# Neighbourhood attention on Trainium2: queries stored rotated by 64 tokens, one unit of work for a whole head

## The chip, the cores and the metric

The kernel is written for one Trainium2 chip and runs on one of its cores. A core has five engines that run at once and meet only through semaphores: TensorE (PE, matrix products and transposes into PSUM; its weight loads are shown as PEld), VectorE (DVE), ScalarE (ACT), GpSimd (POOL) and SyncE (SP, which here issues nearly all transfers). PSUM has eight banks of 2 KB for each of 128 partitions. The metric is the device time of one execution in microseconds, the median of several runs.

## The reference

The model is an encoder of two layers with 512 tokens of width 1024. In each layer three mixers work on the same normalised input: differential attention, a convolution and a two-dimensional neighbourhood attention. Their outputs are gated and merged, and a feed-forward block and a gated embedding follow. The change lies in the neighbourhood attention alone. It sees the 512 tokens as 8 rows of 64 columns; a query at column w attends to all 8 rows, but only to 16 columns around it:

```python
cs = jnp.clip(cols - NA_KC // 2, 0, GRID_W - NA_KC)      # NA_KC = 16, GRID_W = 64
...
s = jnp.einsum('bhwd,bhrwcd->bhwrc', q_r, kn).astype(jnp.float32) * scale
s = s + bias.transpose(0, 2, 1, 3)[None].astype(jnp.float32)
a = jax.nn.softmax(s.reshape(B, HC, GRID_W, KR * NA_KC), axis=-1)
return jnp.einsum('bhwrc,bhrwcd->bhwd', a, vn)
```

There are 8 heads of width 64, and the bias depends on head, row distance and column distance. All is float32.

## The kernel before, in words

Tokens are kept in the order column by column (token = column x 8 + row), so that the 16 columns that a query may see are 128 neighbouring tokens in that order, and a tile of 128 queries (16 columns) sees at most 256 keys. Products that must keep float32 accuracy are made of two or three faster ones: a value is split into a rounded part (by ACT) and the remainder (by DVE), `split` at L162.

PE's instruction order is the order of the program, written by hand. The other engines' orders are laid out by a scheduler that takes what is ready by priority; each queue is then fixed. The dense projections are the bulk of PE's work: `gemm` (L181) multiplies a weight block of 128 x 1024, 8 chunks of three matmuls of 512 columns (L177 to L179), and calls `chunk` after each; every fourth chunk is a tick (L94). The attention's work is cut into generators, called units, that wait in a queue: at a tick, units whose time has come do their next step, and a new unit starts when the one before it has left the gap that `later` gives it (L107). So the short work of a unit stands between ticks' worth of projections.

For each pair of heads `natten_in` (L634) projects queries and keys, makes rounded part and remainder, and has `stack` (L656) copy them by SP's transfers into `st4` and `k2`, where the two parts lie above each other in the partitions, so that two matmuls (`scores`, L809) give a full product. `natten_v` (L665) makes the values of all heads, and at its end copies two 64-token edges of the values into tiles `vd` of their own (L688 to L695).

`natten_unit` (L697) takes two query tiles of one head, so that a head has two units (`half` 0 and 1). The first step makes for each of the two tiles a score tile of 128 x 256 in a PSUM tile `sc` of its own (of two buffers), then DVE adds the bias and takes the maximum (L712, into the bias tile `b`), ACT takes the exponential into `e` with its sum, and after a reciprocal ACT scales `e`. Two of the four query tiles begin their 256 keys at a multiple of 128 tokens (0 and 256), the two in the middle do not (`KEY0` = 0, 64, 192, 256), and those have a 64-column margin of zeros in `e`, written by POOL (L720). Two ticks later the second step transposes the probabilities: five transposes of 128 x 128, the fifth for the edge, into two PSUM tiles that are split into `pp` and `p2`. Two ticks later the third step multiplies by the values: four products of 256 columns with two aligned value tiles and one of 128 columns with the edge tile `vd` (L756), and the output goes into `y`.

Of the kernel before, what the change touches and what calls it, by code (L numbers as in the profile page):

```python
# [11 lines left out]
F32 = mybir.dt.float32  # L12
F32R = mybir.dt.float32r
# [22 lines left out]
KEY0 = (0, 64, 192, 256)  # L36
# [25 lines left out]
class Net:  # L62
# [571 lines left out]
    def natten_in(self, pr, st, ys):  # L634
# [4 lines left out]
        for s, off in enumerate((OFF_QC, OFF_KC)):  # L639
# [16 lines left out]
    def stack(self, nat, low, one, two):  # L656

        for n, part in enumerate((nat, low)):
            for st, r in ((one, 64 * n), (two, 64 - 64 * n)):
                for u in range(2):  # L660
                    if st is not None:
                        self.nc.sync.dma_start(st[r:r + 64, u].bitcast(F32),
                                               part[64 * u:64 * u + 64].bitcast(F32))

    def natten_v(self, st):  # L665
# [31 lines left out]
    def natten_unit(self, pr, half, u, st4, k2, st, y):  # L697

        nc, i = self.nc, self.i
        mm = nc.tensor.matmul  # L700
        head = 2 * pr + u
        b = self.sb("b", [P, 2, NW])
# [3 lines left out]
        m = self.sb("s", [P, 6])  # L706
        for t in range(2):
            qt = 2 * half + t
            sc = self.ps("sc", (P, NW))
            self.scores(sc, st4, k2, u, slice(qt * P, (qt + 1) * P),  # L710
                        slice(KEY0[qt], KEY0[qt] + NW))
            nc.vector.tensor_tensor_reduce(  # L712
                out=b[:, t], in0=sc, in1=b[:, t], scale=-1.0, scalar=3.0e38,
                op0=ALU.add, op1=ALU.min, accum_out=m[:, t:t + 1])
            wide = half != t
            e = self.sb("e", [P, NW + 64 * wide])
            own = slice(64 * (qt == 1), 64 * (qt == 1) + NW)
            if wide:
                pad = slice(0, 64) if qt == 1 else slice(NW, NW + 64)
                nc.gpsimd.memset(e[:, pad], 0.0)  # L720
            self.act(e[:, own], b[:, t], AF.Exp, table="exp", scale=-1.0, bias=m[:, t:t + 1],
                     accum_out=m[:, 2 + t:3 + t])
            es.append((e, e[:, own]))
        nc.vector.reciprocal(m[:, 4:6], m[:, 2:4])
        for t, (_, own) in enumerate(es):
            self.act(own, own, AF.Copy, scale=m[:, 4 + t:5 + t])
        yield 2
        pt = self.ps("tr", (P, 2, 256))
        pt2 = self.ps("tr", (P, P))
        p2 = self.sb("a", [P, P], F32R)  # L730
        for t, (e, _) in enumerate(es):
            qt = 2 * half + t
            c0 = 64 * (qt == 2)
            ts = slice(t * P, (t + 1) * P)
            if qt == 2:
                nc.tensor.transpose(pt2, e[:, 0:P], self.ident)
            for c in range(2):
                nc.tensor.transpose(pt[:, c, ts], e[:, c0 + c * P:c0 + (c + 1) * P], self.ident)
            if qt == 1:
                nc.tensor.transpose(pt2, e[:, NW - 64:NW + 64], self.ident)  # L740
            if half != t:
                ws = ts
        pp = self.sb("pt", [P, 2, 2, 256], F32R)
        self.split(pp[:, 0], pp[:, 1], pt)

        er, eo = (slice(0, 64), slice(64, P))[::1 if half else -1]
        self.split(p2[er], p2[eo], pt2[er])
        yield 2
        vs, vd = st["v", pr // 2]
        av = self.ps(("av", "mm")[u], (P, 256))  # L750
        hc = (pr % 2) * 256 + u * P
        cols = slice(hc, hc + P)
        for n in range(2):
            for k in range(2):
                mm(av, vs[half][:, n, cols], pp[:, k, n], start=n == k == 0, stop=False)
        mm(av[:, ws], vd[:, half, cols], p2, start=False, stop=True)  # L756


        qs = slice(half * 256, half * 256 + 256)
        rs, ro = (slice(0, 64), slice(64, P))[::-1 if u else 1]  # L760
        self.split(y[rs, 0, qs], y[rs, 1, qs], av[rs])
        self.tt(y[rs, 1, qs], y[rs, 1, qs].bitcast(F32), av[ro], ALU.add)
# [46 lines left out]
    def scores(self, out, st4, k2, u, qs, ks):  # L809


        for n, st in enumerate((st4[:, 2 + u], k2[:, u])):
            self.nc.tensor.matmul(out, st4[:, u, qs], st[:, ks], start=n == 0, stop=n == 1)  # L813
# [678 lines left out]
```

## Time and profile before

| | |
|---|---|
| median of 3 runs | 1781.01 us (1780.66 to 1782.22) |
| span of the profiled execution, first to last instruction | 1778.5 us (the page gives no other time of this execution; the median is 2.5 us more) |
| instructions | 27425, of them 10210 matmuls |
| PE / DVE / ACT busy | 1768.7 / 1376.2 / 915.0 us |
| DMA | 256.04 MB, 144 GB/s on average |
| mean granted TensorE clock | 0.999 |

Busy time is the time in which an engine has at least one instruction in hand. Matmuls overlap in the pipeline of PE, so that the distance between two starts, not the printed duration, is what one costs. In timelines the columns are start (us), duration (us), engine, line, operation, written tile <- read tiles, shape, count, and in brackets the idle time before it with what ended it; in the view of windows, the busy time of each engine (with its instructions), granted clock, share of the DMA engines and GB/s. "natten", "diff", "glu" and so on in tile names are the phases of the program.

### The profile page before, as it was taken

To read this page: it belongs to the slowest core of one execution; us is meant where nothing else is said; L and a number is where in the kernel's file an instruction comes from. 1 tells how busy PE (TensorE), PEld (TensorE's weight loads), DVE (VectorE), ACT (ScalarE), POOL (GpSimd) and SP (SyncE) were. 2 spreads that over 40 slices of the span, in tenths; PEclk is the share of its full clock that TensorE was granted. 3 is DMA by queue.
4 is the path that set the end of the run, shared out by engine and by line. 5 is a ranking of instruction groups with operands and counts; after the bars stand their busy time and mean duration, and the time that the engine had idled before them with its cause. 6 is when DMAs were issued, how large, how long until landed. Compare 5 with 4: busy or idle time off the path is not lost.

```text
span 1778.5 us, 27425 instructions
## 1 busy us (share of the span) xinstructions
PE 1768.7 (99%) x10210; PEld 1559.0 (88%) x10210; DVE 1376.2 (77%) x2284; ACT 915.0 (51%) x1607; POOL 108.8 (6%) x146
## 2 busy tenths in 40 slices
PE   9999999999999999999999999999999999999998
PEld 7888888888899899998888888888888998989987
DVE  7878887998787576777776788889887875766676
ACT  5577545325576254454545765452356652634544
POOL 0000000000121010100000000000001210101000
PEclk9999999999999999999999999999999999999999
DMA  5666541334767365543447655423256663655332
GB/s 210 188 183 171 161 125 44 111 98 146 224 160 182 116 168 152 141 121 126 141 127 197 177 166 149 113 71 95 94 177 197 173 178 112 176 140 154 99 104 95
DMA packets 113507, 256.04 MB, mean 144 GB/s; under 512 B 14560, under 2 KB 19424, under 8 KB 113376
## 3 DMA queue, kind: packets, MB, share of 16 engines
q1 hardware_dynamic: 99984, 229.93, 42.2%
q0 software_dynamic: 12672, 23.07, 7.8%
q8 instruction: 80, 1.31, 0.3%
q10 hardware_dynamic: 720, 1.31, 0.2%
q14 instruction: 51, 0.42, 0.1%
HBM read 215.46 MB, written 7.34 MB: 125 GB/s over the span
## 4 chain that ended last, share of the span: by engine, by line
PE 95%; DVE 2%; ACT 1%; issue 1%; DMA 0%; POOL 0%; ACTq 0%; POOLq 0%; DVEq 0%
PE ffn_mm L177 4%; PE ffn_mm L178 4%; PE ffn_mm L179 4%; PE ffn_mm L1022 3%; PE ffn_mm L1020 3%; PE ffn_mm L1021 3%; PE ffn_sc L1020 3%; PE ffn_sc L1022 3%; PE ffn_sc L1021 3%; PE mergea_mm L179 2%; PE mergea_mm L177 2%; PE mergea_mm L178 2%; PE diff_sc L813 2%; PE gatec_mm L177 2%; PE gatec_mm L178 2%; PE gatec_mm L179 2%
## 5 line engine op out<-in xcount | busy, mean ns | idle before, releaser
L160 DVE SCALAR_TENSOR_TENSOR conv_z<-glu_z,pre_par,conv_z 128x512 f32<-128x512 f32 x240 | 179.6, 748 | 3.3
L143 ACT ACTIVATE ffn_wh<-ffn_wr 128x1024 fp32r<-128x1024 f32 (+1 forms) x92 | 93.4, 1021 | 140.2 <-PE ffn_mm L178 75.3
L157 DVE TENSOR_TENSOR ffn_wl<-ffn_wr,ffn_wh 128x1024 fp32r<-128x1024 f32 (+1 forms) x92 | 107.6, 1175 | 40.7 <-ACT ffn_wh L143 40.3
L990 POOL DMA_DIRECT2D ffn_qk<-w_fu x88 | 78.0, 961 | 601.7 <-DMA ffn_qk<-w_fu 336.4
L157 DVE TENSOR_TENSOR ffn_t<-ffn_mm,wo_rb 128x512 f32<-128x512 f32 (+1 forms) x86 | 47.8, 556 | 71.0 <-PE ffn_mm L179 60.7
L143 ACT ACTIVATE mergea_wh<-mergea_wr 128x1024 fp32r<-128x1024 f32 (+1 forms) x32 | 27.1, 846 | 96.8 <-PE mergea_mm L178 79.5
L157 DVE TENSOR_TENSOR ffn_wl<-ffn_qk,ffn_wh 128x1024 fp32r<-128x1024 f32 x44 | 53.9, 1224 | 15.5 <-ACT ffn_wh L143 15.5
L143 ACT ACTIVATE ffn_wh<-ffn_qk 128x1024 fp32r<-128x1024 f32 x44 | 46.6, 1060 | 33.3 <-PE ffn_mm L178 16.1
L143 ACT ACTIVATE diff_a<-diff_sc,diff_s 128x512 f32<-128x512 f32 x32 | 22.0, 687 | 61.0 <-DVE diff_s L905 61.0
L177 PE MATMUL ffn_mm<-ffn_v,ffn_wh 128*128 128x512 f32 x132 | 51.4, 389 | 0.0
L178 PE MATMUL ffn_mm<-ffn_v,ffn_wh 128*128 128x512 f32 x132 | 51.4, 389 | 0.0
L179 PE MATMUL ffn_mm<-ffn_v,ffn_wl 128*128 128x512 f32 x132 | 51.3, 389 | 0.0
L177 PE MATMUL ffn_mm<-ffn_y,ffn_wh 128*128 128x512 f32 x132 | 51.3, 389 | 0.0
L178 PE MATMUL ffn_mm<-ffn_y,ffn_wh 128*128 128x512 f32 x132 | 51.3, 389 | 0.0
L179 PE MATMUL ffn_mm<-ffn_y,ffn_wl 128*128 128x512 f32 x132 | 51.3, 389 | 0.0
L1020 PE MATMUL ffn_mm<-wo_h,ffn_wh 128*128 128x256 f32 x176 | 49.9, 284 | 0.0
L1021 PE MATMUL ffn_sc<-wo_h,ffn_wh 128*128 128x256 f32 x176 | 49.8, 283 | 0.0
L1022 PE MATMUL ffn_mm<-wo_h,ffn_wl 128*128 128x256 f32 x176 | 49.8, 283 | 0.0
L1022 PE MATMUL ffn_sc<-wo_h,ffn_wl 128*128 128x256 f32 x176 | 49.8, 283 | 0.0
L1020 PE MATMUL ffn_sc<-wo_h,ffn_wh 128*128 128x256 f32 x176 | 49.8, 283 | 0.0
L1021 PE MATMUL ffn_mm<-wo_h,ffn_wh 128*128 128x256 f32 x176 | 49.8, 283 | 0.0
L143 ACT ACTIVATE natten_wh<-natten_wr 128x1024 fp32r<-128x1024 f32 x24 | 25.4, 1058 | 41.4 <-issue 15.2
(868 smaller groups left out, 6548.5 us busy)
## 6 DMA issues: line engine op xcount, KB each, us to landing
ffn_qk<-w_fu POOLq DMA_DIRECT2D x88, 256.0 KB, 6.5
ffn_wr<-w_fg SPq DMA_DIRECT2D x44, 512.0 KB, 4.2
ffn_wr<-w_fd SPq DMA_DIRECT2D x32, 448.0 KB, 3.9
ffn_r<-w_fu SPq DMA_DIRECT2D x44, 256.0 KB, 3.2
ffn_qk<-w_fg SPq DMA_DIRECT2D x44, 256.0 KB, 2.9
ffn_qk<-w_fu SPq DMA_DIRECT2D x44, 256.0 KB, 3.2
natten_wr<-w_in SPq DMA_DIRECT2D x16, 512.0 KB, 4.4
natten_b<-bias SPq DMA_DIRECT2D x32, 256.0 KB, 4.0
```

What stands on the lines that cost most here:

```text
L143: i = self.nc.scalar.activation(out, in_, func, **kw)
L157: return self.nc.vector.tensor_tensor(out, a, b, op)
L160: return self.nc.vector.scalar_tensor_tensor(out, a, s, b, op0, op1)
L177: mm(out, wh, ah, start=first, stop=False, **kw)
L178: mm(out, wh, al, start=False, stop=False, **kw)
L179: mm(out, wl, ah, start=False, stop=last, **kw)
L813: self.nc.tensor.matmul(out, st4[:, u, qs], st[:, ks], start=n == 0, stop=n == 1)
L990: nc.gpsimd.dma_start(q, wu[:, lo], accum_op=ALU.add)
L1020: mm(out, wh[:, c], bh, start=first and k == 0, stop=False, skip_group_check=True)
L1021: mm(out, wh[:, c], bl, start=False, stop=False, skip_group_check=True)
L1022: mm(out, wl[:, c], bh, start=False, stop=k == 3, skip_group_check=True)
```

## The change

Queries are stored rotated by 64 tokens (`MOVE`): tile q of the rotated order holds tokens 128 q - 64 to 128 q + 63, taken round the end. A tile then needs two key tiles of 128 that begin at multiples of 128: tiles q - 1 and q for q = 1, 2, 3, and tiles 0 and 3 for q = 0, which holds the first and the last 64 tokens. The bias table is laid out to match, on the host. There are no edge tiles any more, neither of values (`vd`) nor of probabilities (`p2`), and no margins.

- `stack` writes the queries in two pieces each (448 and 64 columns), the keys as before.
- A unit takes a whole head; a pair of heads has two units with a gap of two ticks instead of four with a gap of one. Its second step comes three ticks after the first, instead of two, and the third two ticks after that.
- The first step makes four score tiles, two in each PSUM tile `sc` of 2 x 256, that is one 2 KB bank; only the first product into a bank starts an accumulation. DVE's work on tile t = 0 stands in the program ahead of the scores of t = 1. The exponential is written over the biased scores, in the bias tile. The second bias tile of a unit has the tag `e`, of which there are four buffers; the first has `b`, with two.
- The second step makes eight transposes into two PSUM tiles of four. The third makes eight value products, two for each key tile, of 192, 256, 256 and 192 columns, into one PSUM tile of 512 columns in the order of the tokens (so the rotation ends here), and one split of 64 x 512.
- `scores` takes a function that picks the keys; for tile 0 it is the first and the last 128 of 512.

```diff
-KEY0 = (0, 64, 192, 256)
+MOVE = 64
...
-            self.stack(nat, low, st4[:, 2 * s:2 * s + 2], k2 if s else None)
+            self.stack(nat, low, st4[:, 2 * s:2 * s + 2], k2 if s else None, 0 if s else MOVE)
         ys.append(self.sb("y", [P, 2, 512], F32R))
-        for n in range(4):
-            self.later(self.natten_unit(pr, n // 2, n % 2, st4, k2, st, ys[pr]), 6 if pr == 3 else 5 if pr else 10, 1)
+        for u in range(2):
+            self.later(self.natten_unit(pr, u, st4, k2, st, ys[pr]), 6 if pr == 3 else 5 if pr else 10, 2)
...
+        cols = (slice(0, 512 - move), slice(move, 512)), (slice(512 - move, 512), slice(0, move))
...
+                    for src, dst in cols[:1 + (move > 0)]:
+                        if st is not None:
+                            self.nc.sync.dma_start(st[r:r + 64, u, dst].bitcast(F32),
+                                                   part[64 * u:64 * u + 64, src].bitcast(F32))
...
-        for g in range(2):
-            vd = self.sb("x", [P, 2, 512], F32R)
-            for n, edge in enumerate((vs[g][1][0:64, 0], vs[g][0][64:P, 1])):
-                for o in range(0, P, 64):
-                    self.nc.sync.dma_start(vd[o:o + 64, n].bitcast(F32), edge.bitcast(F32))
-            st["v", g] = vs[g], vd
+        st.update(enumerate(vs))
...
+        bs = [self.sb(t, [P, 2, NW]) for t in ("b", "e")]
         with self.tc.high_priority(offset=100):
-            nc.sync.dma_start(b, self.a["bias"][i, head, half])
+            for half, b in enumerate(bs):
+                nc.sync.dma_start(b, self.a["bias"][i, head, half])
...
+        for half, b in enumerate(bs):
+            sc = self.ps("sc", (P, 2, NW))
+            for t in range(2):
+                qt = 2 * half + t
+                keys = (lambda a, qt=qt: a[:, qt * P - P:qt * P + P]) if qt else \
+                    (lambda a: a.rearrange("p (a b) -> p a b", b=P)[:, 0::3])
+                self.scores(sc[:, t] if qt else sc[:, t].rearrange("p (a b) -> p a b", b=P),
+                            st4, k2, u, slice(qt * P, (qt + 1) * P), keys, t == 0,
+                            skip_group_check=True)
+                es.append(b[:, t])
+                nc.vector.tensor_tensor_reduce(
+                    out=b[:, t], in0=sc[:, t], in1=b[:, t], scale=-1.0, scalar=3.0e38,
+                    op0=ALU.add, op1=ALU.min, accum_out=m[:, qt:qt + 1])
+                self.act(b[:, t], b[:, t], AF.Exp, table="exp", scale=-1.0, bias=m[:, qt:qt + 1],
+                         accum_out=m[:, 4 + qt:5 + qt])
+            c = slice(4 + 2 * half, 6 + 2 * half)
+            nc.vector.reciprocal(m[:, c], m[:, c])
+            for t in range(2):
+                self.act(b[:, t], b[:, t], AF.Copy, scale=m[:, c][:, t:t + 1])
+        yield 3
+        ps = []
+        for half in range(2):
+            pt = self.ps("tr", (P, 4, P))
+            for n in range(4):
+                kc, q = 2 * half + n // 2, (2 * half + (n + 1) // 2) % 4
+                c = (kc != q - 1 if q else kc == 3) * P
+                nc.tensor.transpose(pt[:, n], es[q][:, c:c + P], self.ident)
+            pp = self.sb("pt", [P, 2, 512], F32R)
+            self.split(pp[:, 0], pp[:, 1], pt.rearrange("p a b -> p (a b)"))
+            ps.append(pp)
         yield 2
...
+        for kc, (o, n, c) in enumerate(((0, 192, MOVE), (MOVE, 256, 256), (192, 256, 0), (320, 192, 256))):
             for k in range(2):
-                mm(av, vs[half][:, n, cols], pp[:, k, n], start=n == k == 0, stop=False)
-        mm(av[:, ws], vd[:, half, cols], p2, start=False, stop=True)
+                mm(av[:, o:o + n], vs[kc // 2][:, kc % 2, hc:hc + P], ps[kc // 2][:, k, c:c + n],
+                   start=kc == k == 0, stop=kc == 3 and k == 1, skip_group_check=True)
...
-    def scores(self, out, st4, k2, u, qs, ks):
+    def scores(self, out, st4, k2, u, qs, keys, first=True, **kw):
         for n, st in enumerate((st4[:, 2 + u], k2[:, u])):
-            self.nc.tensor.matmul(out, st4[:, u, qs], st[:, ks], start=n == 0, stop=n == 1)
+            self.nc.tensor.matmul(out, st4[:, u, qs], keys(st), start=first and n == 0, stop=n == 1, **kw)
```

More of the change, by code (lines that the diff above doesn't have):

```diff
@@ L701, in natten_unit @@
         head = 2 * pr + u
-        b = self.sb("b", [P, 2, NW])
+        bs = [self.sb(t, [P, 2, NW]) for t in ("b", "e")]
         with self.tc.high_priority(offset=100):
-            nc.sync.dma_start(b, self.a["bias"][i, head, half])
+            for half, b in enumerate(bs):
+                nc.sync.dma_start(b, self.a["bias"][i, head, half])
+        m = self.sb("s", [P, 8])
         es = []
[L706 to L723, printed above, removed]
@@ L724, in natten_unit @@
-        nc.vector.reciprocal(m[:, 4:6], m[:, 2:4])
-        for t, (_, own) in enumerate(es):
-            self.act(own, own, AF.Copy, scale=m[:, 4 + t:5 + t])
-        yield 2
[L728 to L750, printed above, removed]
+        for half, b in enumerate(bs):
[17 more added lines that the diff above has]
+                self.act(b[:, t], b[:, t], AF.Copy, scale=m[:, c][:, t:t + 1])
@@ L751, in natten_unit @@
+        yield 2
+        av = self.ps(("av", "mm")[u])
         hc = (pr % 2) * 256 + u * P
-        cols = slice(hc, hc + P)
-        for n in range(2):
+        vs = st[pr // 2]
+        for kc, (o, n, c) in enumerate(((0, 192, MOVE), (MOVE, 256, 256), (192, 256, 0), (320, 192, 256))):
             for k in range(2):
-                mm(av, vs[half][:, n, cols], pp[:, k, n], start=n == k == 0, stop=False)
-        mm(av[:, ws], vd[:, half, cols], p2, start=False, stop=True)
-        qs = slice(half * 256, half * 256 + 256)
+                mm(av[:, o:o + n], vs[kc // 2][:, kc % 2, hc:hc + P], ps[kc // 2][:, k, c:c + n],
+                   start=kc == k == 0, stop=kc == 3 and k == 1, skip_group_check=True)
@@ L760, in natten_unit @@
         rs, ro = (slice(0, 64), slice(64, P))[::-1 if u else 1]
-        self.split(y[rs, 0, qs], y[rs, 1, qs], av[rs])
-        self.tt(y[rs, 1, qs], y[rs, 1, qs].bitcast(F32), av[ro], ALU.add)
+        self.split(y[rs, 0], y[rs, 1], av[rs])
+        self.tt(y[rs, 1], y[rs, 1].bitcast(F32), av[ro], ALU.add)
     def gate_c(self, acc, m):
@@ L903, in probs @@
             sc = self.ps("sc")
-            self.scores(sc, st4, k2, u, qs, slice(0, 512))
+            self.scores(sc, st4, k2, u, qs, lambda a: a)
             nc.vector.tensor_reduce(out=m[:, u:u + 1], in_=sc, op=ALU.max, axis=AX.X, negate=True)
```

12 lines of the change are left out of this document (5 added, 7 removed).

## The prediction

> **What bounds the kernel now.** I read the profile's page first.
>
> ```profile
> span 1778.5 us, 27425 instructions
> ...
> PE 1768.7 (99%) x10210; PEld 1559.0 (88%) x10210; DVE 1376.2 (77%) x2284; ACT 915.0 (51%) x1607; POOL 108.8 (6%) x146
> ...
> PE 95%; DVE 2%; ACT 1%; issue 1%; DMA 0%; POOL 0%; ACTq 0%; POOLq 0%; DVEq 0%
> ```
>
> TensorE (PE) is busy 99% of the span and is 95% of the chain that ended last. A busy PE need not be a fast one, so I looked next for time in which it waits. In the list of PE's waits these are the two largest that concern other engines in mid-kernel (total us, times, longest):
>
> ```profile
> PE ffn_mm L1022 <- DVE ffn_pt L157: 2.0, 2, 1.0
> ...
> PE natten_tr L738 <- ACT natten_e L143: 0.3, 2, 0.2
> ```
>
> So next to nothing is lost to waiting, least of all in the neighbourhood attention (natten), and what decides is how long PE's own instruction stream is, plus any wait that the change puts into it. VectorE (DVE), ScalarE (ACT) and the queues matter only where PE waits for them. For PE I use the distance from one start to the next, since the printed durations overlap. The timeline of PE around the first natten units (start us, us):
>
> ```profile
> 83.35 0.60 PE L738 MATMUL natten_tr<-pre_ident,natten_e 128*128 128x128 f32 x4
> 83.78 0.27 PE L740 MATMUL natten_tr<-pre_ident,natten_e 128*128 128x128 f32 x1
> 83.81 0.36 PE L813 MATMUL natten_sc<-natten_qk 128*128 128x256 f32 x1
> 84.01 0.28 PE L813 MATMUL natten_sc<-natten_x,natten_qk 128*128 128x256 f32 x1
> ...
> 84.25 0.28 PE L813 MATMUL natten_sc<-natten_x,natten_qk 128*128 128x256 f32 x1
> 84.37 0.39 PE L177 MATMUL glu_mm<-glu_h,glu_wh 128*128 128x512 f32 x1
> 84.60 0.39 PE L178 MATMUL glu_mm<-glu_h,glu_wh 128*128 128x512 f32 x1
> ...
> 91.41 0.29 PE L736 MATMUL natten_tr<-pre_ident,natten_e 128*128 128x128 f32 x1
> 91.53 0.60 PE L738 MATMUL natten_tr<-pre_ident,natten_e 128*128 128x128 f32 x4
> 91.89 0.48 PE L177 MATMUL natten_mm<-glu_h,natten_wh 128*128 128x512 f32 x1
> 92.21 0.39 PE L178 MATMUL natten_mm<-glu_h,natten_wh 128*128 128x512 f32 x1
> ...
> 98.70 0.64 PE L755 MATMUL natten_av<-natten_pt,natten_v 128*128 128x256 f32 x4
> 99.17 0.22 PE L756 MATMUL natten_av<-natten_a,natten_x 128*128 128x128 f32 x1
> 99.23 0.46 PE L177 MATMUL natten_mm<-glu_h,natten_wh 128*128 128x512 f32 x1
> 99.53 0.40 PE L178 MATMUL natten_mm<-glu_h,natten_wh 128*128 128x512 f32 x1
> ```
>
> A 512-column matmul takes 0.23 us (84.37 to 84.60) and a 256-column one 0.12 (84.25 to 84.37). The 128-wide one at 99.17 starts its successor after 0.06, but that successor then needs 0.30 instead of 0.23: together 0.36, so the narrow one really costs 0.13. Fewer columns than 256 buy nothing in these rows.
>
> **What leaves PE.** Per head the old code has two units, each with five transposes and five value products.
>
> Transposes: the first five run from 83.35 to 84.01, less one score matmul of 0.12: 0.54. The other five run from 91.41 to 92.21, less 0.23: 0.57. Ten cost 1.11. The new unit does eight in a row, which the softmax attention (diff) already does:
>
> ```profile
> 1070.89 1.03 PE L861 MATMUL diff_tr<-pre_ident,diff_a 128*128 128x128 f32 x8
> 1071.68 0.48 PE L177 MATMUL diff_mm<-ple_h,diff_wh 128*128 128x512 f32 x1
> 1071.99 0.40 PE L178 MATMUL diff_mm<-ple_h,diff_wh 128*128 128x512 f32 x1
> ```
>
> 1070.89 to 1071.99, less 0.23, is 0.87. Saved: 0.24 us a head.
>
> Value products: five take 98.70 to 99.53, less 0.23: 0.60, so 1.20 a head. The new unit has eight: four of 256 columns (0.47, as 98.70 to 99.17) and four of 192, a width that the trace does not have. From below, scaled by columns, one is 192/256 x 0.12 = 0.09; from above it is 0.13, like the 128-wide one. I take 0.12, since its neighbours on either side are at that. Saved: 1.20 - 0.47 - 0.48 = 0.25 a head, between 0.21 and 0.37. The Trainium skill, page "TensorE: Matmul & The Clock Gate", section "Back-to-back issue gap", puts the distance at columns / 2.4 plus 2.5 ns, 82 ns for 192; its section "LDWEIGHTS (loading the stationary operand)" puts a load of 128 columns at 107 ns. By the first alone the sum below would be about 2.4 us lower (64 x 0.038), by the second as it stands; the row of the 128-wide matmul sides with the second.
>
> Score matmuls: eight of 256 columns a head before and after. Two of them read the keys in two pieces of 128 columns; I take 0 for that, since as many columns go through, and from above another 0.12 each, as if each piece were a matmul: 3.8 us in all. Together 0.49 us a head, x 16 heads (8 in each of 2 layers) = **7.8 us saved**, bounds 16 x 0.45 = 7.2 and 16 x 0.61 = 9.8.
>
> **What is put into PE's stream.** In the old unit each score tile is a PSUM tile of its own. In the new one two share one tile of 2 x 256 float32, one 2 KB bank, and the program's order is scores of t = 0, DVE's bias-add-and-maximum of t = 0, scores of t = 1, the same of t = 1. Whether the second score matmul may start while DVE reads the other half of the bank decides this case. No PE write stands in that position in the trace, but ACT and DVE do, in the values' eviction (L687): two column halves of one accumulator, each copied by ACT and then subtracted by DVE, into different SBUF tiles.
>
> ```profile
> 953.92 0.38 ACT L143 ACTIVATE natten_v<-natten_sc 128x256 fp32r<-128x256 f32 x1
> ...
> 955.26 0.41 DVE L157 TENSOR_TENSOR natten_v<-natten_sc,natten_v 128x256 fp32r<-128x256 f32 x1
> ...
> 955.71 0.39 ACT L143 ACTIVATE natten_v<-natten_sc 128x256 fp32r<-128x256 f32 x1 [1.41 <-DVE natten_v L157]
> ```
>
> ACT does half 0 at 953.92, then sits idle 1.41 us until DVE has finished half 0 (955.26 + 0.41 = 955.67), and does half 1 at 955.71. It needs nothing of DVE's there but the bank. So this program's waits keep two engines out of one bank even where columns differ, and I take it that PE is kept out too. The Trainium skill, page "PSUM — Partial Sum Buffer", section "PSUM bank collisions raise a hardware error", asks for just that: guard by bank, not by address, since a matmul write beside another engine's access fails even on other columns. No run here shows what happens without the guard; by this rule the waits below are due, and a guard by address would leave only the saving.
>
> The wait has the following price. The trace around a unit whose scores were served at once:
>
> ```profile
> 80.13 0.28 PE L813 MATMUL natten_sc<-natten_qk 128*128 128x256 f32 x1
> 80.24 0.28 PE L813 MATMUL natten_sc<-natten_x,natten_qk 128*128 128x256 f32 x1
> ...
> 80.56 0.42 DVE L712 CUSTOM_DVE_ANT_0 natten_b<-natten_sc,natten_b 128x256 f32<-128x256 f32 x1
> 80.91 0.08 DVE L712 DVE_READ_ACCUMULATOR2_ANT natten_s<- 128x1 f32 x1
> 80.91 0.42 DVE L712 CUSTOM_DVE_ANT_0 natten_b<-natten_sc,natten_b 128x256 f32<-128x256 f32 x1
> ...
> 81.03 0.51 ACT L143 ACTIVATE natten_e<-natten_b,natten_s 128x256 f32<-128x256 f32 x1 [0.16 <-DVE natten_s L712]
> ```
>
> DVE starts 0.32 after the second score matmul (80.24 to 80.56), is done 0.43 later (80.99), and a waiting engine goes on 0.04 after that (81.03). First half of a unit: the next score matmul comes 0.79 after the one at 80.24, not 0.12: 0.67 lost. Second half: its first scores go into the other bank and follow at once on those of t = 1, so counted from the first matmul of t = 1 PE has issued four in 0.47; DVE starts t = 1 at 0.12 + 0.32 = 0.44, half 1's first tile 0.35 later (80.56 to 80.91), ends it at 0.79 + 0.43 = 1.22, and PE goes on at 1.26: 0.79 lost. That is 1.46 a head if DVE is free at once, x 16 = 23.4 us.
>
> DVE is not always free. Behind the unit at 83.81 it came late, and this is how full it is in that stretch (PE, PEld, DVE, ACT, POOL busy):
>
> ```profile
> 84.41 1.22 DVE L157 TENSOR_TENSOR natten_wl<-natten_wr,natten_wh 128x1024 fp32r<-128x1024 f32 x1 [2.09 <-ACT natten_wh L143]
> ...
> 86.60 0.42 DVE L712 CUSTOM_DVE_ANT_0 natten_b<-natten_sc,natten_b 128x256 f32<-128x256 f32 x1
> ...
> 100.00:125.00 25.00, 25.00 (x139) 21.57 (x138) 19.36 (x48) 17.55 (x43) 0.61 (x4) 1.00 0.65 176
> ```
>
> 19.36 of 25 us is 77%. Half of the longest instruction (1.22) met 77% of the time is 0.47, half of the mean one (19.36/48 = 0.40) is 0.16. I take 0.4 a wait, as the long ones hold most of the time; from below 0 (80.56), from above one whole 1.22. The 2.3 us late at 86.60 I leave out: there transposes of another unit fell into the same step and DVE split them first, and in the new spacing (scores at ticks 0 and 2, transposes at 3 and 5) they do not. Two waits a head: 0.8 more, x 16 = 12.8, between 0 and 39.
>
> Behind PE's waiting score matmul stand the rest of the unit's scores and then the projection's matmuls; ACT and DVE wait for those in turn, but neither is the bound, so the loss counts once. A wait this long has no cover: PE issues in the written order.
>
> **What costs nothing.** DVE, ACT and POOL lose work (32 memsets, the second small split, half the instructions of the output split): PE does not wait for it now. The bias tile is now overwritten in place and kept until the transposes, which frees the `b` buffer later, but the next unit that uses it is a projection pair (7 ticks of some 3.3 us, as 76.9 to 80.1) further on, so its load still comes early; if that cover went, a load's 4 us would stand ahead of the unit's first maximum, where PE now waits. The query stack becomes 8 DMA issues a head pair instead of 4; 8 copies of the value edge go each layer:
>
> ```profile
> L662 SPq DMA_DIRECT2D natten_qk<-natten_kh x32: 461/468/1164, 52.4 to 1013.0; - x32
> ```
>
> At 0.47 us each that is 1.9 us of SP's queue more per head pair, ahead of weight loads that are requested three buffers early; if it all reached PE, 8 x 1.9 = 15 us.
>
> **Sum.** 23.4 + 12.8 - 7.8 = +28.4 us on the span of 1778.5: 1806.9. The page gives no other time of that execution; the median of the timed runs, 1781.0, is 2.5 us above the span, which I add: **1809 us**. Ends: 23.4 - 9.8 = +13.6 (1795) and 23.4 + 39 - 7.2 + 3.8 = +59 (1840).
>
> **Rivals.**
> No wait on PE: matmuls write one half of the bank while DVE reads the other. Only the saving is left: 1781.0 - 7.8 = 1773, faster. For it: the trace has no PE write to a bank that DVE is reading, so the wait itself is inferred. Against it: ACT's 1.41 us. It decides from the point where the waits cost less than 0.49 us a head, 0.24 each; the floor I find is 0.67.
> DVE serves at once every time, because at a unit's first step it mostly idles: +15.6, 1797. For it: 80.56; against: 77% busy.
> DVE is a whole weight split late at each wait: up to 1840. For it: 86.60; against: the transposes are out of the way.
> SP's longer queue delays weights on top of the waits: 1809 + 15 = 1824. Against: no PE wait for a weight among the waits now.
> The change doing less than it says (192 columns at 0.13) is the 7.2 above and changes the sum by 0.6.
>
> **Chances.** Forecast 0.55, DVE at once 0.14, DVE later 0.13, SP 0.03: slower 0.85. No wait 0.12: faster. Waits near their break-even, within 0.2% (3.6 us, about what a measurement here can tell from none): 0.03. The range 1794 to 1834 holds the slower cases but for the far end of the late one.
>
> **What would show it.** Right: in the list of PE's waits, the natten score matmuls wait on DVE's bias-add-and-maximum some 32 times, 0.7 to 1.2 us each, 30 us or more in all; PE's instruction count falls by 16 x 4 = 64 (two transposes and two value products a head); the clock stays near full. Wrong: score matmuls of a natten unit that run eight in a row at 0.12 us, or waits of PE on a bias or weight load.

## The result, and the profile after

The changed kernel takes 1835.6 us (median of 4 runs, 1834.2 to 1836.5) against 1781.1 before: a ratio of 1.0305, 95% interval 1.0290 to 1.0319. It is slower, as forecast, but by 54 us where 28 were forecast, and the time lies just outside the range of 1794 to 1834.

The page of the kernel after (span; busy time of the engines; shares of the chain that ended last):

```profile
span 1834.5 us, 27101 instructions
...
PE 1785.8 (97%) x10146; PEld 1568.3 (85%) x10146; DVE 1362.4 (74%) x2220; ACT 904.0 (49%) x1559; POOL 103.9 (6%) x114
...
PE 90%; DVE 6%; ACT 2%; issue 1%; DMA 1%; SPq 0%; POOL 0%; POOLq 0%; ACTq 0%; DVEq 0%
```

PE executes 64 instructions fewer than before (10210 to 10146), and yet it is busy 17 us longer. DVE, ACT and POOL are all busy for less time, but DVE now has 6% of the chain, where it had 2%. The list of PE's waits (total us, times, longest) says where:

```profile
PE natten_sc L794 <- DVE natten_s L713: 38.8, 32, 4.4
PE ffn_mm L1003 <- DVE ffn_pt L157: 2.0, 2, 1.0
...
PE diff_sc L794 <- ACT diff_e L143: 0.8, 2, 0.4
```

The first row is new: the score matmuls of t = 1 wait for DVE's maximum of t = 0, twice in each of 16 heads. Counted as in the prediction, from start to start less the 0.12 us of a score matmul, these 32 waits cost 44.1 us. One unit, first PE, then DVE (start us, us, and in brackets the idle time and what ended it):

```profile
78.01 0.28 PE L794 MATMUL natten_sc<-natten_x,natten_qk 128*128 128x256 f32 x1
78.82 0.39 PE L794 MATMUL natten_sc<-natten_qk 128*128 128x256 f32 x1 [0.53 <-DVE natten_s L713]
...
79.29 0.28 PE L794 MATMUL natten_sc<-natten_x,natten_qk 128*128 128x256 f32 x1
80.98 0.39 PE L794 MATMUL natten_sc<-natten_qk 128*128 128x256 f32 x1 [1.42 <-DVE natten_s L713]
...
81.55 0.40 PE L178 MATMUL natten_mm<-glu_h,natten_wh 128*128 128x512 f32 x1
...
82.50 0.63 PE L178 MATMUL natten_mm<-glu_h,natten_wh 128*128 128x512 f32 x1
82.93 0.63 PE L179 MATMUL natten_mm<-glu_h,natten_wl 128*128 128x512 f32 x1
```

```profile
78.33 0.42 DVE L713 CUSTOM_DVE_ANT_0 natten_b<-natten_sc,natten_b 128x256 f32<-128x256 f32 x1 [1.01 <-PE natten_sc L794]
...
79.01 1.23 DVE L157 TENSOR_TENSOR natten_wl<-natten_wr,natten_wh 128x1024 fp32r<-128x1024 f32 x1 [0.25 <-ACT natten_wh L143]
80.15 0.42 DVE L713 CUSTOM_DVE_ANT_0 natten_b<-natten_sc,natten_b 128x256 f32<-128x256 f32 x1
...
80.50 0.42 DVE L713 CUSTOM_DVE_ANT_0 natten_e<-natten_sc,natten_e 128x256 f32<-128x256 f32 x1
```

First wait: 78.01 to 78.82 less 0.12 is 0.69, the floor. Second: 79.29 to 80.98 less 0.12 is 1.57, twice its floor of 0.79. While PE was held by the first wait, DVE came to a weight split of 1.23 us; behind it stood the maximum of t = 1, and behind that the one that PE waits for (natten_e, 80.50).

The last two PE rows show the second thing: a 512-column matmul that takes 0.23 us elsewhere takes 0.43 (82.50 to 82.93). By windows (window, length; busy us and count of PE, PEld, DVE, ACT, POOL; granted clock; DMA share; GB/s):

```profile
73.00:78.00 5.00, 5.00 (x24) 4.14 (x23) 4.21 (x9) 2.10 (x6) 0.00 (x0) 1.00 0.24 68
78.00:82.00 4.00, 2.06 (x12) 1.54 (x11) 3.42 (x12) 3.34 (x9) 0.00 (x0) 0.99 0.28 86
82.00:85.00 3.00, 3.00 (x8) 2.32 (x7) 0.79 (x2) 1.94 (x6) 0.00 (x0) 0.50 0.69 215
```

In the 3 us behind the two waits the granted clock is 0.50. The view of the cores has the mean granted clock of the whole execution:

```profile
core 0: 1834.5 us, clock 0.989
```

against 0.999 before, on average. 1834.5 x 0.011 - 1778.5 x 0.001 = 18.4 us, give or take 1 for the rounding of each clock. Taken one by one, the trace has eleven stretches of 3.41 us at 0.50 between its start and its end, which cost PE half their length, 18.8 us. They lie behind nine of the 16 heads only. The first unit of the second layer has the same two waits as the unit shown, 0.53 and 1.42 us by the brackets, and behind them the clock stays full (PE, window):

```profile
990.21 0.39 PE L794 MATMUL natten_sc<-natten_qk 128*128 128x256 f32 x1 [1.42 <-DVE natten_s L713]
```

```profile
991.00:994.00 3.00, 3.00 (x15) 2.46 (x14) 1.12 (x5) 2.77 (x10) 0.00 (x0) 1.00 0.96 243
```

So the size of the waits alone doesn't decide; the last section comes back to it.

Waits 44.1 + clock 18.4 - the forecast saving 7.8 = 54.7; the spans differ by 56.0.

### The profile page after: what moved, and what is told of

It reads as the page before. It is cut to its first block, busy times and chain, and to the rows that moved or that the text cites. A ratio compares the mean times of both kernels' runs of the same rounds, so it can differ in the third digit from the quotient of the medians.

```text
span 1834.5 us, 27101 instructions
## 1 busy us (share of the span) xinstructions
PE 1785.8 (97%) x10146; PEld 1568.3 (85%) x10146; DVE 1362.4 (74%) x2220; ACT 904.0 (49%) x1559; POOL 103.9 (6%) x114
## 4 chain that ended last, share of the span: by engine, by line
PE 90%; DVE 6%; ACT 2%; issue 1%; DMA 1%; SPq 0%; POOL 0%; POOLq 0%; ACTq 0%; DVEq 0%
PE ffn_mm L179 4%; PE ffn_mm L177 4%; PE ffn_mm L178 4%; PE ffn_mm L1003 3%; PE ffn_mm L1001 3%; PE ffn_mm L1002 3%; PE ffn_sc L1001 3%; PE ffn_sc L1003 3%; PE ffn_sc L1002 3%; PE mergea_mm L178 2%; PE mergea_mm L177 2%; PE mergea_mm L179 2%; PE gateb_mm L178 2%; PE gateb_mm L179 2%; PE gateb_mm L177 2%; PE diff_sc L794 2%
## 5 line engine op out<-in xcount | busy, mean ns | idle before, releaser
L794 PE MATMUL natten_sc<-natten_qk 128*128 128x256 f32 x64 | 21.7, 349 | 38.8 <-DVE natten_s L713 38.8
L157 DVE TENSOR_TENSOR diff_wl<-diff_wr,diff_wh 128x1024 fp32r<-128x1024 f32 x24 | 29.4, 1223 | 30.5 <-ACT diff_wh L143 24.7
L794 PEld LDWEIGHTS natten_sc<-natten_qk 128*128 128x128 f32 x64 | 12.5, 196 | 45.8 <-DVE natten_s L713 45.4
L1002 PE MATMUL ffn_sc<-wo_h,ffn_wh 128*128 128x256 f32 x176 | 49.8, 283 | 0.0
```

Of the source, the lines that this page charges most:

```text
L157: return self.nc.vector.tensor_tensor(out, a, b, op)
L794: self.nc.tensor.matmul(out, st4[:, u, qs], keys(st), start=first and n == 0, stop=n == 1, **kw)
L1002: mm(out, wh[:, c], bl, start=False, stop=False, skip_group_check=True)
```

## The experiments

My theory: the bank that two score tiles share costs the 32 waits, DVE's order of work makes them late, and PE's idle time lowers the clock behind them. Its rivals: the waits come from something else in the new unit (the whole head, the rotation's transfers), the lower clock from transfers or from more work.

**e1_scores_first.** After, with both tiles of a bank written before DVE reads either.

```diff
                 self.scores(..., t == 0, skip_group_check=True)
+            for t in range(2):
+                qt = 2 * half + t
                 es.append(b[:, t])
                 nc.vector.tensor_tensor_reduce(...)
```

> The changed kernel with only the order of the scores changed: both score tiles of a bank are written before VectorE reads the first. Theory (the 56 us of span come from PE waiting for the bank, 44 us in 32 waits, and from a halved clock after those waits, about 18 us, against about 8 us saved): no wait of a score matmul on VectorE is left, the clock is back at 0.999, and the time is 1781 - 8 = 1773 us. Rival (something else in the longer unit costs time: the two-piece key reading, the query copies, a unit of twice the length): the waits go, but the time stays above 1781 us, or the clock stays at 0.99.

1780.9 us (11 runs), ratio 1.0000 (0.9991 to 1.0009), clock 0.998. The 32 waits are gone, and the time falls by 55 us. The 1773 us that I expected aren't reached: the saving over the kernel before doesn't show. Two new waits of PE stand in the list:

```profile
PE diff_sc L796 <- ACT diff_e L143: 5.7, 2, 3.4
```

PE, then DVE of this kernel around the first of them:

```profile
174.59 1.07 PE L741 MATMUL natten_mm<-natten_pt,natten_v 128*128 128x192 f32 x8
175.51 0.42 PE L796 MATMUL diff_sc<-diff_qk 128*128 128x512 f32 x1
...
178.40 0.50 PE L796 MATMUL diff_sc<-diff_qk 128*128 128x512 f32 x1 [2.23 <-ACT diff_e L143]
```

```profile
170.82 0.68 DVE L888 TENSOR_REDUCE diff_s<-diff_sc 128x1 f32<-128x512 f32 x1
173.24 0.69 DVE L157 TENSOR_TENSOR diff_rp<-diff_rp,diff_r 128x512 f32<-128x512 f32 x1 [1.73 <-DMA diff_rp<-diff_rp]
...
176.85 0.68 DVE L888 TENSOR_REDUCE diff_s<-diff_sc 128x1 f32<-128x512 f32 x1
```

DVE's order puts rope work for the next differential head between the two maxima of the first (L888). That work stands still for a transfer (1.73 us), so the second maximum comes 6 us after the first, ACT's exponentials come late, and PE, which is further ahead than it was, waits for their bank. The first row gives the size of a saved piece: eight value products take 174.59 to 175.51, 0.92.

**e2_one_bank_before.** Before, with nothing changed but that the two score tiles of a unit share one bank (so that only the first product into it starts an accumulation).

```diff
+        both = self.ps("sc", (P, 2, NW))
...
-            sc = self.ps("sc", (P, NW))
+            sc = both[:, t]
...
```

> The kernel before with one thing of the change alone: the two score tiles of a unit share one bank, in the same interleaved order. 32 units, one wait each. Theory (the bank makes the wait): 32 waits on VectorE of at least 0.67 us, with 0.4 to 1 us of lateness, so 34 to 50 us: 1815 to 1831 us if the clock holds at 0.999 because each wait stands alone, 3 us or more from the next. Rival (the clock falls with the total of idle time, however spread): clock 0.99 and about 18 us more. Rival (the bank is not the cause): 1781 us.

1833.4 us, ratio 1.0294 (1.0279 to 1.0310), clock 0.993. The list of its waits:

```profile
PE natten_sc L814 <- DVE natten_s L713: 36.8, 32, 3.0
```

The old half-head unit, with its unrotated queries and its margins, gets 32 such waits too, 42.0 us from start to start, and nearly the same time. Packing two tiles into one bank is the cause; it needs nothing else of the change. In all these kernels two tiles that share a bank are also halves of one PSUM tile of the program, so no run tells whether PE is kept out of the bank or out of that tile. The clock missed what I expected: it fell to 0.993 though each wait stands alone, and the time lies above the 1815 to 1831 that a full clock would have given.

**e3_halves_apart.** After, with one step of projection work between the two halves of a head.

```diff
-        yield 3
+            yield 1 + half
```

> The changed kernel with the two halves of a unit's scores one tick apart, so that the two waits of a unit lie some 3 us from each other; transposes stay three ticks after the start. Theory (the clock falls where two waits stand within one stretch of some 3 us): 32 waits of 0.67 us and up, 40 us or so in all, but the clock back at about 0.999: 1781 - 8 + 40 = 1813 us. Rival (any wait of this length lowers the clock, or the clock has another cause): clock 0.99 and about 1830 us.

1830.0 us, ratio 1.0273 (1.0259 to 1.0287), clock 0.993. The waits, start to start, total 44.3 us, as in the kernel after, but they lie differently: seven of the first eight of each layer are at the floor of 0.69, most of the others at 1.8 to 3.0. I had expected the low clock to go, because no two waits stand together any more; it rose from 0.989 to 0.993 only. One wait, here of 2.80 us, can be enough (PE of this kernel):

```profile
142.20 0.58 PE L794 MATMUL natten_sc<-natten_qk 128*128 128x256 f32 x1 [2.80 <-DVE natten_s L713]
...
143.22 0.63 PE L178 MATMUL diff_mm<-glu_h,diff_wh 128*128 128x512 f32 x1
143.65 0.63 PE L179 MATMUL diff_mm<-glu_h,diff_wl 128*128 128x512 f32 x1
```

**e4_filled_waits.** After, with three 512-column matmuls on zeros, 0.68 us of work that nobody reads, in each wait.

```diff
+        spare = self.ps("tr")
...
+                for _ in range(3 * t):
+                    mm(spare, self.zero_r, self.zero_r[:, None, :].to_broadcast([P, 4, P]),
+                       start=True, stop=True)
```

> The changed kernel with three 512-column matmuls on zeros (0.68 us) put into each of the 32 waits, into a PSUM bank that nobody reads: extra work for PE that fits into the shortest wait (0.68). Theory (idle time of PE lowers the clock): the ends of the waits stay where they are, idle time falls by 32 x 0.68 = 22 us, the clock is back at 0.999 and the time falls by most of 18 us, to about 1817 us, although PE does more. Rival (the clock is not a matter of PE's idle time): 1835 us or more, clock 0.989.

1820.7 us, ratio 1.0225 (1.0211 to 1.0239): 15 us faster than the kernel after, though 96 matmuls were added. The gaps between the scores of t = 0 and t = 1 add up to 44.1 us, exactly as in the kernel after; only what PE does in them differs. The rows of this kernel (waits; the window behind the same unit; clock):

```profile
PE natten_sc L798 <- DVE natten_s L717: 16.9, 16, 3.3
```

```profile
82.00:85.00 3.00, 3.00 (x15) 2.49 (x14) 0.15 (x1) 0.91 (x2) 0.00 (x0) 1.00 0.79 264
core 0: 1818.9 us, clock 0.998
```

The clock stays at 1.00 with a DMA share of 0.79, above the 0.69 of the slowed window after, so the transfers aren't what lowers it. Of the eleven stretches at 0.50 two are left. Same gaps, less idle time, 15 us: this is the price of the clock, taken by itself.

**e5_two_ticks and e6_diff_later.** Two ways to move the differential head's maxima in e1_scores_first. e5: the transposes one step earlier. e6: the differential unit two steps later.

```diff
e5:
-        yield 3
+        yield 2
e6:
-            self.later(self.natten_unit(...), 6 if pr == 3 else 5 if pr else 10, 2)
+            self.later(self.natten_unit(...), 6 if pr == 3 else 5 if pr else 10,
+                       4 if pr == 3 and u else 2)
```

> Both score tiles of a bank are written before VectorE reads either (as in e1_scores_first), and a unit's transposes come two steps of the order after its scores instead of three. In VectorE's order the two maxima of the first differential head then stand next to each other, ahead of the rope work that waits for a transfer. Theory (the 8 us that the shorter transposes and value products save are there in e1_scores_first, and the two new waits for diff_e, 5.7 us, took them back): waits for diff_e back to at most 1 us, waits for natten_s none, span 1770 to 1773, time 1772 to 1776, ratio about 0.996. Rival (the saving was never there, or the earlier transposes wait for the softmax instead): 1781, ratio 1.000, with a new wait in the transposes if the second.

1776.7 us, ratio 0.9973 (0.9964 to 0.9983), a little above the 1772 to 1776 expected. The waits for diff_e are gone from the top of the list, but both sides were partly right: the earlier transposes now wait for the softmax.

```profile
PE natten_tr L731 <- ACT natten_e L143: 2.1, 6, 0.5
```

> As e1_scores_first, but the last neighbourhood head of a layer is followed by four steps instead of two before the next unit starts, so the first differential head's scores come as late as in the kernel before. Theory as for e5_two_ticks: the waits for diff_e shrink from 5.7 us to under 1 us and the time falls to 1773 to 1777. Rival (the wait follows VectorE's order, in which one piece of rope work still stands ahead of the first maximum, and not the start of the scores): waits of 3 to 6 us remain, time about 1780.

1773.8 us, ratio 0.9957 (0.9945 to 0.9970), clock 1.000. This version beats both kernels. Its remaining wait at that place, and PE's transposes:

```profile
PE diff_sc L797 <- ACT diff_e L143: 0.9, 2, 0.5
```

```profile
87.96 0.49 PE L732 MATMUL natten_tr<-pre_ident,natten_b 128*128 128x128 f32 x3
...
89.07 0.40 PE L178 MATMUL glu_mm<-glu_h,glu_wh 128*128 128x512 f32 x1
```

Eight transposes cost 1.11 - 0.23 = 0.88 and the products 0.92, so a head is 0.23 + 0.28 = 0.51 us shorter, 8.2 us in all by the rows of these heads; the time is 7.3 us below the kernel before.

**e7_maxima_together and e9_splits_last.** After, with six weight splits (those like the one at 79.01) moved on DVE only: in e7 behind the bank's second maximum, in e9 behind the first maximum of the second half.

```diff
+SECOND = {174: 1, 185: 5, 322: 29, 1532: 33, 1543: 37, 1680: 61}      (e7)
+LAST = {174: 2, 185: 6, 322: 30, 1532: 34, 1543: 38, 1680: 62}        (e9)
...
             self.low = self.split(hi[:, :n], lo[:, :n], raw[:, :n])
+            if self.uid in SECOND:
+                self.behind(self.low, self.maxima[SECOND[self.uid]])
```

> The kernel after, but six weight splits on VectorE (three in each layer) that fell between the two maxima of a bank are ordered behind the second one; nothing else is moved. Theory (these splits of 1.23 us are what makes the second-half waits late, and a pair of waits that adds up to over 2 us is what lowers the clock behind it): the six following waits of 1.5 to 1.8 us fall to 0.8 to 1.0, the sum of the waits falls from 44.1 by 4 to 5 us, the clock behind these six pairs stays full for another 6 to 9 us, time 1821 to 1827. Rival 1 (lateness follows from VectorE's load as a whole, other work takes the place of the splits): no change, 1834 to 1837. Rival 2 (the clock doesn't follow the size of a pair of waits): 1830 to 1832.

1839.2 us, ratio 1.0316 (1.0297 to 1.0336), clock 0.986 in the profiled run. The four runs lie between 1833.8 and 1842.6 us, with clocks of 0.991 to 0.985, so no difference from the kernel after is shown. My reading of which maximum matters was wrong. The split still stood ahead of the second half's first maximum, which the second wait is for, and that wait grew from 1.57 to 1.99 us.

> As e7_maxima_together, but the six weight splits stand behind the first maximum of the second half, the one that the unit's second wait is for, and not just behind the second maximum of the first half, where e7_maxima_together put them ahead of exactly that one. Theory (these splits of 1.23 us are the lateness of the second wait in six heads, and a pair of waits of 2.3 us in all lowers the clock behind it while a pair of 1.5 us does not): in these six heads the waits are 0.68 and 0.80, the sum of the 32 waits falls from 44.1 to about 39, no halved clock behind these six pairs, time 1821 to 1828. Rival 1 (other work on VectorE takes their place): 1834 to 1838. Rival 2 (the clock falls behind short pairs too): waits 39, clock as in the kernel after, 1829 to 1832.

1822.8 us, ratio 1.0234 (1.0219 to 1.0249), clock 0.993. The unit that is shown above for the kernel after, now in e9 (PE, DVE, windows):

```profile
78.62 0.28 PE L798 MATMUL natten_sc<-natten_x,natten_qk 128*128 128x256 f32 x1
79.54 0.38 PE L798 MATMUL natten_sc<-natten_qk 128*128 128x256 f32 x1 [0.63 <-DVE natten_s L717]
```

```profile
79.06 0.42 DVE L717 CUSTOM_DVE_ANT_0 natten_e<-natten_sc,natten_e 128x256 f32<-128x256 f32 x1
...
79.40 1.22 DVE L159 TENSOR_TENSOR natten_wl<-natten_wr,natten_wh 128x1024 fp32r<-128x1024 f32 x1
```

```profile
77.00:81.00 4.00, 2.84 (x15) 2.20 (x14) 2.73 (x11) 3.29 (x9) 0.00 (x0) 1.00 0.35 119
81.00:84.00 3.00, 3.00 (x15) 2.47 (x14) 1.36 (x5) 2.04 (x6) 0.00 (x0) 1.00 0.67 207
```

The second wait is 0.80, its floor, and the clock behind it stays at 1.00. The 32 waits add up to 38.6 us, 5.5 less, of which 4.9 are in these six second waits, and the span is 13.8 shorter. So the splits were the lateness here. The clock accounts for most of the other 8 us: the stretches of 3.41 us at 0.50 fall from eleven to seven, worth 6.8 us. Behind the six heads there were five and none is left; of the other heads, two lost theirs and three, whose waits hardly changed, got one. Part of this is thus where the waits happen to fall.

**e8_products_256.** e1_scores_first with all value products 256 columns wide; 64 columns too many are added in, so the output isn't the reference's.

```diff
-        for kc, (o, n, c) in enumerate(((0, 192, MOVE), (MOVE, 256, 256), (192, 256, 0), (320, 192, 256))):
+        for kc, (o, n, c) in enumerate(((0, 256, 0), (MOVE, 256, 256), (192, 256, 0), (256, 256, 256))):
```

> As e1_scores_first, but all eight value products of a head are 256 columns wide; the first and the last two then take 64 columns more than belong to them, so the output differs from the reference's. Theory (as the prediction had it, a 192-column product costs what a 256-column one costs, 0.12 us): eight products of a head span 0.94 to 0.96 us from first to last start plus one, as with 192; time within 1 us of e1_scores_first. Rival (cost goes by columns): the four 192-column products were 0.03 us shorter each, so 0.12 us more per head now, 1.9 us in all.

PE's value products in this kernel, as above for e1_scores_first:

```profile
175.86 1.11 PE L741 MATMUL natten_mm<-natten_pt,natten_v 128*128 128x256 f32 x8
176.81 0.40 PE L796 MATMUL diff_sc<-diff_qk 128*128 128x512 f32 x1
```

0.95 us against 0.92 (0.91 in most other heads): a 192-column product is 0.03 / 4 to 0.04 / 4, about 0.01 us, shorter than a 256-column one. The one time, 1773.8 us, can't be set against e1_scores_first: the other widths changed DVE's planned order too, the differential head's two maxima came next to each other, and the wait for diff_e left the list. Its DVE row there, two maxima in one go:

```profile
172.07 1.28 DVE L888 TENSOR_REDUCE diff_s<-diff_sc 128x1 f32<-128x512 f32 x2
```

**e10_query_whole.** e6_diff_later with the queries stacked unrotated; each row of scores belongs to a query 64 tokens off, so the output isn't the reference's.

```diff
-            self.stack(nat, low, st4[:, 2 * s:2 * s + 2], k2 if s else None, 0 if s else MOVE)
+            self.stack(nat, low, st4[:, 2 * s:2 * s + 2], k2 if s else None)
```

> As e6_diff_later, but the natten queries are stacked unrotated, by four transfers for each of two parts instead of eight; each row of scores then belongs to a query 64 tokens off, so the output differs from the reference's. Theory (the rotation's transfers are hidden behind other work, as the prediction had it): same time as e6_diff_later within 2 us, 1772 to 1776. Rival (the longer queue on SyncE delays other loads, among them the rope transfer that VectorE waits for near 171 us and 1051 us): 3 to 6 us faster, 1768 to 1771.

1773.3 us, ratio 0.9957 (0.9940 to 0.9974), as e6_diff_later. The rotation's transfers cost nothing.

**e11_own_banks.** After, with each score tile in a PSUM tile of its own, the two buffers taken in turn.

```diff
-            sc = self.ps("sc", (P, 2, NW))
             for t in range(2):
                 qt = 2 * half + t
+                sc = self.ps("sc", (P, NW))
```

> The kernel after, but each of the four score tiles of a head has a bank of its own out of the same two, taken in turn, and TensorE and VectorE still alternate as in the kernel after. The first two tiles of a head then need no wait, the third waits for the first one's maximum, the fourth for the second one's. Theory (TensorE waits only where it writes into a bank that VectorE has yet to read, and the first wait is shortened by the 0.23 us of the second tile's scores): third tile waits at least 0.68 - 0.23 = 0.45 us, fourth at least 0.1 us, both plus the lateness of VectorE, up to 1.2 us where a weight split comes between; sum of waits 10 to 28 us, most pairs too short to lower the clock, time 1784 to 1808. Rival (the whole head is the cause, whatever the banks): waits near 44 us, 1825 to 1835.

1804.9 us, ratio 1.0134 (1.0119 to 1.0149), clock 0.996. Its waits:

```profile
PE natten_sc L793 <- DVE natten_s L712: 21.0, 20, 3.9
```

12 of the 32 waits are gone: the fourth tile waits in four heads only. The shortest left is 0.45 us start to start, as worked out, and all add up to 24.3. So a whole head of four tiles in two banks costs something too while PE and DVE alternate, but 20 of the 44 us go with the sharing.

## Why the prediction was right or wrong

**The wait itself: right.** PE is kept out of a bank while DVE reads its other half. ACT's 1.41 us in the values' eviction was the right neighbour to go by, and e2_one_bank_before shows it alone, though not whether the bank or the program's tile is what is guarded. The rule of the Trainium skill that stood beside it (page "PSUM — Partial Sum Buffer", section "PSUM bank collisions raise a hardware error") agrees with the 32 waits, which keep PE out of columns that DVE doesn't read; what happens without the guard, no run shows.

**Its floor: right.** 0.67 and 0.79 were forecast; the waits that met a free DVE are 0.68 to 0.69 and 0.79 to 0.80. 23.4 us forecast, 23.5 by these.

**The saving: right.** 7.8 us forecast (0.87 for the transposes, 0.95 for the products); 0.88 and 0.92 measured, 8.2 us, of which the time of e6_diff_later shows 7.3. Of the bounds for 192 columns, the upper end held nearly: about 0.11 us, not 0.09. The formula with 2.5 ns that the prediction cited from the Trainium skill (page "TensorE: Matmul & The Clock Gate", section "Back-to-back issue gap") is given there for an isolated matmul, with the note that at small widths it counts too little in a stream. Here the 0.11 us lie above its 82 ns. The two-piece key reading, taken at 0 and at most 3.8 us, costs nothing: in 14 of the 16 heads of e1_scores_first all eight score matmuls start 0.11 to 0.14 us apart.

**DVE's lateness: the mechanism right, the term too small.** "I take 0.4 a wait" gave 12.8 us; 44.1 - 23.5 = 20.6 were measured, 0.64 a wait, and about half of the waits are longer than the 1.2 us that the prediction gave as their upper end. It is no average over a busy share. By the single waits of the kernel after, 10 us in each of two layers, it lies in a few places of DVE's planned order: in each layer 4.3 us in one head whose maxima stand behind the differential unit's rope work (4.6 and 1.2 us in the first layer), 2.5 in three heads whose second maximum stands behind a weight split, and 3.5 in four waits where output additions and background work come first. e9_splits_last takes the splits' part away, 4.9 of its 5.5 us in both layers. The prediction left the 2.3 us late at 86.60 out as an accident of the old spacing, because of the transposes of another unit. This misread the trace before: what DVE does first there is the weight split at 84.41, which the prediction shows, and the transposes' split comes only behind it:

```profile
85.55 0.69 DVE L157 TENSOR_TENSOR natten_pt<-natten_tr,natten_pt 128x512 fp32r<-128x512 f32 x1
```

So 1.14 of the 2.3 us, 84.41 to 85.55, were a weight split, and weight splits stayed. I should have read what DVE is planned to do at the units' new steps; the planner fills exactly the hole that PE's wait opens between two maxima.

**"The clock stays near full": wrong, and the largest miss.** This is the step that failed: the sum had no term for it; it is about 18 us here. e4_filled_waits, with gaps unchanged, gets 15 of them back. How many of the 32 waits are followed by a low clock is in part luck, as the first units of the two layers show. Nothing in the profile before could give the size, since PE hardly waits there, but a term with bounds was due as soon as 32 waits were added.

**What costs nothing: right.** Bias loads, DVE's smaller work and SP's longer queue appear nowhere among PE's waits; e10_query_whole is 0.5 us from e6_diff_later, inside both intervals. The rivals of SP's queue and of no wait fall. Of the two on DVE, the late one (up to 1840) came nearer the time than my forecast did, but for another reason: the waits alone would have made 1817 (44.1 - 7.8 on 1781), and the clock made the rest.

The corrected sum: 23.5 floor + 20.6 late + 18.4 clock - 8.2 saved = 54.3, for 56.0 of span. The same sum fits three other kernels (waits, clock as above, saving): e7 46.2 + 24.0 - 8.2 = 62.0, measured 61.9; e9 38.6 + 11.0 - 8.2 = 41.4, measured 42.2; e2, without the saving, 42.0 + 11.0 = 53.0, measured 54.0. For e3, e4 and e11 it comes out 2.5, 2.6 and 3.4 us too low, and that is left open.

## What to carry to other kernels

When two tiles are packed into one PSUM bank, write both before another engine reads either; alternating writer and reader put 32 waits into PE's stream here, worth 55 us, and moving the loop's readers behind its writers took all of them out. A wait added to a busy PE can have a second price in the clock behind it, so give it a term of its own, and size lateness from the reader's planned order at that step, not from its busy share. When a saving doesn't arrive, look at the next list of waits: here an unrelated head that came earlier waited it away, and two steps of delay brought it back.

## What the runs showed of the hardware

That the length of a wait alone doesn't decide on the granted clock was new to me. e2_one_bank_before has two waits of the same length, one followed by full speed and one by half (PE; windows):

```profile
89.20 0.39 PE L814 MATMUL natten_sc<-natten_qk 128*128 128x256 f32 x1 [2.79 <-DVE natten_s L713]
...
125.21 0.50 PE L814 MATMUL natten_sc<-natten_qk 128*128 128x256 f32 x1 [2.79 <-DVE natten_s L713]
```

```profile
84.37:87.78 3.41, 2.04 (x13) 1.59 (x11) 1.25 (x2) 3.06 (x6) 0.15 (x1) 1.00 0.90 220
87.78:91.20 3.42, 2.00 (x10) 1.68 (x11) 3.16 (x9) 1.43 (x6) 0.00 (x0) 1.00 0.81 224
121.92:125.33 3.41, 0.62 (x6) 0.42 (x5) 3.26 (x8) 1.60 (x4) 0.15 (x1) 1.00 0.55 114
125.33:128.75 3.42, 3.42 (x10) 2.74 (x11) 0.60 (x3) 1.97 (x6) 0.00 (x0) 0.50 0.79 270
```

In all the traces every stretch at 0.50, except those that the end of the run cuts off, lasts 3.41 us or twice that, and within one trace they start whole multiples of 3.413 us apart: in the kernel after at 81.94, 92.18, 122.90 and 174.10, which is 3, 12 and 27 of them behind the first. I drew the windows above on this grid. The first wait lies across a boundary, with 1.37 us of idle PE on one side and 1.42 on the other; the second lies in one window, which has 2.79. I counted all windows of all 13 traces in this way (idle as in the brackets, where the ends of matmuls are modelled), leaving out those that were at half clock already. All 28 with more than 1.91 us of idle PE were followed by 0.50; of the 29 with 1.52 to 1.91 us, 14 were; of the others, none. So in these runs it is the idle time within one such window that counts, with a band in which the rows don't tell, and the same waits can meet the grid differently. The spread of the four runs of e7_maxima_together may come from that, but only one run of each kernel has a trace, so this isn't shown.

The Trainium skill, page "TensorE: Matmul & The Clock Gate", section "HAM oscillation — how this bites in real kernels", gives the rule as no idle gaps above some 3.4 us; the rows here differ, and less was enough. In the sum of the kernel after, 44 us of gaps thus cost 62. Filling the gaps with matmuls on zeros kept the clock up, and was worth 15 us.

Narrower matmuls gained next to nothing: 192 columns against 256 about 0.01 us of 0.12.
